# A hybrid decoder layer on one core: eight SSD heads' products in one group, the C and B products of four groups in one, and pairs' transposes moved in front of the next scores

## The chip, the core and the metric

The kernel runs on one core of a Trainium2 chip. Its engines are TensorE (PE, matmuls; PEld is its loading of weights), VectorE (DVE), ScalarE (ACT), GpSimd (POOL) and SyncE (SP, which issues most DMAs). Each engine takes its instructions in the order in which they were issued to it, and waits on semaphores for the others. The metric is the device time of one execution in microseconds (us). Before the change the median of three runs is 745.24 us (745.14 to 746.96).

## The reference

One layer, batch 1, 256 positions, width 1024, float32: a SwiGLU block, then a Mamba-2 (SSD) branch and a differential-attention branch side by side, merged by gates, then a second SwiGLU block. What the change touches is inside the two branches:

```
# SSD: 32 heads of 64, 4 groups of 8 heads, chunks of 128 positions
CB     = einsum('bclgn,bcsgn->bgcls', Cc, Bc)            # per group
y_diag = einsum('bgcls,bgecls,bcsgep->bclgep', CB, Lmat, X)
...
# attention: 8 heads, two maps each, values of 128
p    = softmax(s, axis=-1)
attn = p[:, :, 0] - lam * p[:, :, 1]
out  = einsum('bhqk,bkhe->bqhe', attn, v)
out  = rmsnorm(out, subln_g) * (1.0 - lam_init)
y_att = out @ w_branch
```

The kernel takes the two chunks of the SSD branch as one piece of 256 positions with a causal mask, so that its y is one masked product per head.

## The kernel before

Weights come from HBM in chunks of 1 MB (`load_to`, L140), three raw buffers deep. Each is split into a high and a low part in fp32r: ACT casts (`whi`, L168) and DVE subtracts (`wlo`, L171). `take` (L183) keeps the splits two chunks ahead of PE. Products of weights are three fp32r matmuls for one fp32 product (`mm_t` L197 with 256 columns, 48 passes a tile; `mm_nat` L225 with 512 columns, 12 passes a call). Products inside the branches (`pcb`, `py`, `psc`, `po`) and all transposes are plain fp32 matmuls; each shows as two records on PE.

Buffers come from rings by tag: `k4` (29 tiles of 4 KB a partition: split weights, SSD data, V), `k3` (4: the E of the SSD branch, later the scores `s`), `k2` (7). In PSUM, `pj` (3) serves the weight products and `bg` (5) all else.

The middle of the kernel is woven from two strands. The main strand is the weight products: `pbc` and `pxs` (xs, B and C), `pz`, `pq`/`pk`, then `pgt` (gates), `pws` (the SSD branch's output), `pwd` (the attention's output). The second strand is generators in a queue of class `Background` (L1110): after each main call, `back.run(us)` (L1119) takes steps from them until their `yield` values use up the budget; a `BREAK` ends that round early, and what was saved carries over to the next rounds. Until L1173 a scheduler sets the order of the instructions on all engines. From `own_order(PE)` (L1176) on, PE's order is that of the program; on ACT and DVE the scheduler still decides.

The generators that matter here:

- `cb_work` (L862): for each of four groups, one product of C and B (`pcb`: three blocks of 128 columns, L865 and L866) and one masking multiply on DVE into `cbm` (L867). They run among the `pxs` products.
- `ssd_work` (L875): for each group, transposes of xs (`px`, L881) and a multiply with dt into X (L882). Then for each half of four heads (`hf`): a DMA spreads the decay sums over the partitions (`acb`, L890), two E tiles of two heads each are made on ACT and DVE (L898 to L904), and eight products `py` (L913) of E and X follow, held together on PE by manual dependencies. Each product has 64 output rows, so a head takes half of the array. DVE adds `py` to the scaled xs (L921). So there are eight groups of `py` (16 records each) in all.
- `ssd_norm` (L925): gating, group RMS norm and the split into `yh`/`yl`.
- `att_work` (L1078): eight heads in four pairs, six steps n. Step n does `scores` (L979) and `softmax` (L990) of pair n, `turn` (L1018, transposes `pa` and their copy `aT`) of pair n-1's heads, `combine` (L1006) of pair n, `values` (L1027, six products a pair into `po`) and `norm` (L1045) of pair n-1, and `turn` of pair n-2 (L1057: four transposes `pto` of the normalised pair, then the parts `oh` and `ol`).

`Pair.norm` is a chain over three engines: ACT squares `po` into `o` (L1048), DVE reduces it (L1050) and adds the epsilon term (L1051), ACT takes Ln and Exp (L1053, L1054; shown as L261, the helper), DVE multiplies (L1055). `Pair.turn` on PE reads the `o` that the last of these writes.

## Time and profile before

| what | value |
|---|---|
| runs | 745.14, 745.24, 746.96 us |
| profiled execution | 745.16 us, of which 743.4 us are the span from first to last instruction |
| granted PE clock, mean | 0.997 |
| PE's own chain rows | `acc_f` L470 16%, `pup_f` L219 9%, `pg_f` L219 9%, `pws` L234 6%, `pgt` L234 6% |
| DVE, ACT busy | 71%, 59% of the span |
| costliest DVE and ACT groups | `wlo` L171 290.9 us, `whi` L168 247.2 us |
| SSD products `py`, first to last | 306.6 to 374.6 us |
| pairs' transposes `pto`, first to last | 471.1 to 506.0 us |

The page's first part gives each engine's busy time as a share of the span. The chain follows the work that ended last back to what released it, step by step, and sums it by engine. In the timeline, each row starts with the start time and the duration in us, then the engine, the line, the operation, the tile written and the tiles read, and how many instructions the row joins. Matmuls are pipelined: a row's duration reaches past the start of the next row, so the time that a group costs is read from start to start.

### The profile page before, as it was taken

To read this page: it belongs to the slowest core of one execution; us is meant where nothing else is said; L and a number is where in the kernel's file an instruction comes from. 1 tells how busy PE (TensorE), PEld (TensorE's weight loads), DVE (VectorE), ACT (ScalarE), POOL (GpSimd) and SP (SyncE) were. 2 spreads that over 40 slices of the span, in tenths; PEclk is the share of its full clock that TensorE was granted. 3 is DMA by queue.
4 is the path that set the end of the run, shared out by engine and by line. 5 is a ranking of instruction groups with operands and counts; after the bars stand their busy time and mean duration, and the time that the engine had idled before them with its cause. 6 is when DMAs were issued, how large, how long until landed. Compare 5 with 4: busy or idle time off the path is not lost.

```text
span 743.4 us, 11055 instructions
## 1 busy us (share of the span) xinstructions
PE 734.7 (99%) x4369; PEld 641.3 (86%) x4369; DVE 524.9 (71%) x807; ACT 441.3 (59%) x742; POOL 37.8 (5%) x72
## 2 busy tenths in 40 slices
PE   8999999999999999999999999999999999999996
PEld 6888888888889999999999888888888888888885
DVE  7986567654577888767888998684774867766612
ACT  6665557543566565957967666782664655665512
POOL 2700000000200000000000000000010000000000
PEclk9999999999999999999999999999999999999998
DMA  8884676486253647574656555364470767644701
GB/s 297 225 265 152 206 227 254 174 281 226 64 170 116 202 140 233 168 221 148 197 174 218 173 175 210 127 236 189 135 241 22 226 227 227 190 172 183 277 1 56
DMA packets 94212, 137.96 MB, mean 186 GB/s; under 512 B 2684, under 2 KB 68304, under 8 KB 94160
## 3 DMA queue, kind: packets, MB, share of 16 engines
q1 hardware_dynamic: 91488, 129.51, 52.9%
q0 software_dynamic: 2368, 7.22, 3.2%
q8 instruction: 34, 0.56, 0.3%
q10 hardware_dynamic: 304, 0.53, 0.2%
q14 instruction: 18, 0.15, 0.1%
HBM read 136.17 MB, written 1.08 MB: 185 GB/s over the span
## 4 chain that ended last, share of the span: by engine, by line
PE 98%; DMA 0%; DVE 0%; issue 0%; ACT 0%; DVEq 0%
PE acc_f L470 16%; PE pup_f L219 9%; PE pg_f L219 9%; PE pws L234 6%; PE pgt L234 6%; PE pg_f L218 4%; PE pup_f L218 4%; PE pn_f L244 3%; PE pn_f L234 3%; PE acc_mx L470 3%; PE pn_mx L234 3%; PE pwd L234 3%; PE pz L207 2%; PE pxs L207 2%; PE pz L205 2%; PE pz L204 2%
## 5 line engine op out<-in xcount | busy, mean ns | idle before, releaser
L171 DVE TENSOR_TENSOR wlo<-raw,whi 128x1024 fp32r<-128x1024 f32 (+1 forms) x246 | 290.9, 1211 | 55.7 <-ACT whi L168 54.6
L168 ACT CAST whi<-raw 128x1024 fp32r<-128x1024 f32 (+1 forms) x245 | 247.2, 1047 | 55.3 <-PE acc_f L470 21.7
L219 PE MATMUL pg_f<-u_f,whi 128*128 128x512 f32 x288 | 101.3, 396 | 0.0
L219 PE MATMUL pup_f<-u_f,whi 128*128 128x512 f32 x288 | 101.1, 396 | 0.0
L218 PE MATMUL pg_f<-u_f,wlo 128*128 128x256 f32 x252 | 70.6, 280 | 0.0
L218 PE MATMUL pup_f<-u_f,wlo 128*128 128x256 f32 x252 | 70.3, 279 | 0.0
L219 PEld LDWEIGHTS pg_f<-u_f,whi 128*128 128x128 f32 x288 | 52.8, 188 | 9.7
L219 PEld LDWEIGHTS pup_f<-u_f,whi 128*128 128x128 f32 x288 | 52.7, 188 | 9.8
L470 PE MATMUL acc_f<-whi,gh_f 128*128 128x512 f32 x176 | 58.1, 390 | 0.0
L470 PE MATMUL acc_f<-whi,gl_f 128*128 128x512 f32 x176 | 58.1, 389 | 0.0
L470 PE MATMUL acc_f<-wlo,gh_f 128*128 128x512 f32 x176 | 58.1, 389 | 0.0
L218 PEld LDWEIGHTS pg_f<-u_f,wlo 128*128 128x128 f32 x252 | 47.5, 189 | 1.7
L218 PEld LDWEIGHTS pup_f<-u_f,wlo 128*128 128x128 f32 x252 | 47.5, 189 | 1.6
L223 DVE TENSOR_TENSOR su_f<-pup_f,su_f 128x256 f32<-128x256 f32 x36 | 15.2, 421 | 40.5 <-ACT su_f L222 40.5
L470 PEld LDWEIGHTS acc_f<-wlo,gh_f 128*128 128x128 f32 x176 | 33.0, 188 | 6.9
L470 PEld LDWEIGHTS acc_f<-whi,gl_f 128*128 128x128 f32 x176 | 33.0, 188 | 6.8
L470 PEld LDWEIGHTS acc_f<-whi,gh_f 128*128 128x128 f32 x176 | 33.0, 188 | 6.7
L234 PE MATMUL pgt<-whi,u_mx 128*128 128x512 f32 x128 | 33.1, 393 | 0.0
L222 ACT COPY su_f<-pup_f 128x256 f32<-128x256 f32 x36 | 13.4, 371 | 31.4 <-PE pup_f L219 31.2
L204 PE MATMUL pxs<-u_mx,whi 128*128 128x256 f32 x128 | 31.7, 285 | 0.0
L204 PE MATMUL pz<-u_mx,whi 128*128 128x256 f32 x128 | 31.6, 284 | 0.0
L205 PE MATMUL pz<-u_mx,whi 128*128 128x256 f32 x128 | 31.4, 283 | 0.0
(310 smaller groups left out, 1433.6 us busy)
## 6 DMA issues: line engine op xcount, KB each, us to landing
raw<-in_w_in_dram SPq DMA_DIRECT2D x40, 1024.0 KB, 5.4
raw<-in_ffn_w_down_dram SPq DMA_DIRECT2D x22, 1024.0 KB, 5.1
raw<-in_ffn_w_gate_dram SPq DMA_DIRECT2D x20, 1024.0 KB, 6.0
raw<-in_ffn_w_up_dram SPq DMA_DIRECT2D x20, 1024.0 KB, 5.4
raw<-in_ssd_w_branch_dram SPq DMA_DIRECT2D x8, 1024.0 KB, 5.1
acb<-acd POOLq DMA_DIRECT2D x8, 512.0 KB, 4.9
raw<-in_da_w_branch_dram SPq DMA_DIRECT2D x4, 1024.0 KB, 5.1
raw<-in_w_out_dram SPq DMA_DIRECT2D x4, 1024.0 KB, 4.9
```

The lines of the kernel that those rows point to most:

```text
L168: copy(hi[:, js, :], r[:, q * nj + j:q * nj + j + n, :])
L171: nc.vector.tensor_sub(lo[:, js, :], r[:, q * nj + j:q * nj + j + n, :], hi[:, js, :].bitcast(F32))
L204: nc.tensor.matmul(acc[m], wh(j)[:, cs], ah(k0 + j), start=first and j == ks[0], stop=False)
L205: nc.tensor.matmul(acc[m], wh(j)[:, cs], al(k0 + j), start=False, stop=False)
L207: nc.tensor.matmul(acc[m], wl(j)[:, cs], ah(k0 + j), start=False, stop=last and j == ks[-1])
L218: nc.tensor.matmul(acc[:, :T], wl(j)[:, cs], ah(j), start=False, stop=False)
L219: nc.tensor.matmul(acc, wh(j)[:, cs], ahl(j), start=j == 0, stop=j == KD - 1)
L222: nc.scalar.copy(dst[:, m, :], acc[:, T:])
L223: nc.vector.tensor_tensor(dst[:, m, :], acc[:, :T], dst[:, m, :], ALU.add)
L234: nc.tensor.matmul(acc, a(k0 + j), b(j), start=first and i == 0, stop=last and i == 11)
L244: nc.tensor.matmul(accs[b], x_(k0 + j), w_(j), start=first and j == 0 and w_ is wh and x_ is acts[b][0], stop=last and j == 3 and w_ is wl)
L470: nc.tensor.matmul(acc[b][q], x_[:, ts], w_(kt)[:, halves[q]], start=i == 0 and kt == 0 and x_ is ah and w_ is wh, stop=i == n - 1 and kt ...
```

## The change

Three edits. `cb_work` issues the four groups' products in one go, chained by manual dependencies, into four PSUM tiles, and then does the four multiplies. `ssd_work` makes the E of both halves first and then issues the products of all eight heads of a group, chained, last pair first, with two `py` tiles; the four additions follow, and the `yield` values are 4 x 1.4 and 1.6 instead of 2 x (2 x 1.4 + 0.8). `att_work` runs `turn` of pair n-2 at the start of step n, directly before the scores, instead of at its end; its `yield 0.8` goes, and the yields after each softmax are 2.7 from n = 2 on.

```diff
     def cb_work():
-        for g in range(4):
-            pc = bg([P, 3 * P], f"pcb{g}")
-            nc.tensor.matmul(pc[:, P:], bT[:, g, :P], cT[:, g, :], start=True, stop=True)
-            nc.tensor.matmul(pc[:, :P], bT[:, g, P:], cT[:, g, P:], start=True, stop=True)
+        pcs = [bg([P, 3 * P], f"pcb{g}") for g in range(4)]
+        last = None
+        for g, pc in enumerate(pcs):
+            for m in (nc.tensor.matmul(pc[:, P:], bT[:, g, :P], cT[:, g, :], start=True, stop=True),
+                      nc.tensor.matmul(pc[:, :P], bT[:, g, P:], cT[:, g, P:], start=True, stop=True)):
+                if last is not None:
+                    tc.add_manual_dep(m.ins, last.ins.name, order, reason="together")
+                last = m
+        for g, pc in enumerate(pcs):
             nc.vector.tensor_tensor(cbm[g], pc, m3.rearrange("p a b -> p (a b)"), ALU.mult)
             yield 0.5
...
+            Es = []
             for hf in range(2):
                 acb = k4([P, 4, T], f"acb{g}{hf}")
                 r0 = g * 8 + hf * 4
                 nc.gpsimd.dma_start(acb, acd[r0:r0 + 4, :].partition_broadcast(P))
-                py = bg([P, 2, T], f"py{g}{hf}")
-                Es = []
                 for pr in range(2):
                     E = k3([P, 2, 3 * P], f"E{g}{hf}{pr}")
...
                     yield 1.4

-                last = None
-                for pr in (1, 0):
-                    for keys in range(2):
-                        for i in range(2):
-                            xc = slice((hf * 4 + pr * 2 + i) * 64, (hf * 4 + pr * 2 + i + 1) * 64)
-                            o = py[i * 64:(i + 1) * 64, pr, keys * P:]
-                            m = nc.tensor.matmul(o, X[:, keys, xc], Es[pr][:, i, (1 - keys) * P:(3 - 2 * keys) * P],
-                                                 start=keys == 0, stop=keys == 1)
-                            if last is not None:
-                                tc.add_manual_dep(m.ins, last.ins.name, order, reason="together")
-                            last = m
-                for pr in range(2):
-                    c = hf * 2 + pr
-                    dc = 96 + g * 4 + c
-                    nc.vector.scalar_tensor_tensor(xs[g][:, c, :], xs[g][:, c, :], cols_b[:, dc:dc + 1],
-                                                   py[:, pr, :], ALU.mult, ALU.add)
-                yield 0.8
+            py = [bg([P, 2, T], f"py{g}{hf}") for hf in range(2)]
+            last = None
+            for c in (3, 2, 1, 0):
+                for keys in range(2):
+                    for i in range(2):
+                        xc = slice((c * 2 + i) * 64, (c * 2 + i + 1) * 64)
+                        o = py[c // 2][i * 64:(i + 1) * 64, c % 2, keys * P:]
+                        m = nc.tensor.matmul(o, X[:, keys, xc], Es[c][:, i, (1 - keys) * P:(3 - 2 * keys) * P],
+                                             start=keys == 0, stop=keys == 1)
+                        if last is not None:
+                            tc.add_manual_dep(m.ins, last.ins.name, order, reason="together")
+                        last = m
+            for c in (3, 2, 1, 0):
+                dc = 96 + g * 4 + c
+                nc.vector.scalar_tensor_tensor(xs[g][:, c, :], xs[g][:, c, :], cols_b[:, dc:dc + 1],
+                                               py[c // 2][:, c % 2, :], ALU.mult, ALU.add)
+            yield 1.6
...
             here, old = heads[2 * n:2 * n + 2], heads[2 * n - 2:2 * n] if n else []
+            if n >= 2:
+                pairs[n - 2].turn()
             for head in here:
                 head.scores()
             for head in here:
                 head.softmax()
-                yield 2.3
+                yield 2.3 if n < 2 else 2.7
...
                 yield 1.8
                 if n == H_ATT // 2:
                     yield BREAK
-            if n >= 2:
-                pairs[n - 2].turn()
-                yield 0.8
```

## The prediction

> **What bounds the kernel now.** First the page: busy time and the chain that ended last.

> ```profile
> span 743.4 us, 11055 instructions
> ...
> PE 734.7 (99%) x4369; PEld 641.3 (86%) x4369; DVE 524.9 (71%) x807; ACT 441.3 (59%) x742; POOL 37.8 (5%) x72
> ...
> PE 98%; DMA 0%; DVE 0%; issue 0%; ACT 0%; DVEq 0%
> ```

> PE is busy in 99% of the span and the chain of waits is PE for 98% of it. There is no slack on PE to gain from, and whatever PE waits for newly is added whole. So I read the change as a change of PE's program: what each group of matmuls costs beside its neighbours, and which operand each group would have to wait for. For that I used the timeline of PE, and for the operands the timeline of all engines. PE issues strictly in its order; from before the gate products on, that order is the program's own, written by `own_order(PE)`.

> **SSD heads, eight together.** PE's timeline around the first two `py` groups (columns: start us, duration us, group):

> ```profile
> 306.05 0.52 PE L207 MATMUL pz<-u_mx,wlo 128*128 128x256 f32 x3
> 306.68 1.52 PE L913 MATMUL py<-E,X 128*64 128x256 f32 x16
> 308.13 0.86 PE L207 MATMUL pz<-u_mx,wlo 128*128 128x256 f32 x5
> 308.83 0.28 PE L204 MATMUL pz<-u_mx,whi 128*128 128x256 f32 x1
> ...
> 310.75 1.12 PE L207 MATMUL pz<-u_mx,wlo 128*128 128x256 f32 x8
> 311.80 1.52 PE L913 MATMUL py<-E,X 128*64 128x256 f32 x16
> ```

> An undisturbed f32r pass of 256 columns takes 0.12 (308.83 to 310.75 is 16 of them). After 306.05 three passes need 0.36, so `py` could start at 306.41; it started at 306.68, 0.27 later. After 310.75 eight passes need 0.96, to 311.71; `py` started at 311.80, 0.09 later. So entering the half-array form costs 0.09, and the first group also waited 0.18 for its E. Leaving costs 0.10: five passes from 308.13 to 308.83 take 0.70 instead of 0.60. A group takes 1.45 itself (306.68 to 308.13).

> The next rows give what the same number of fp32 columns takes in the full form:

> ```profile
> 248.84 0.60 PE L865 MATMUL pcb<-cT,bT 128*128 128x256 f32 x2
> 249.28 0.38 PE L866 MATMUL pcb<-cT,bT 128*128 128x128 f32 x2
> 249.42 0.36 PE L204 MATMUL pxs<-u_mx,whi 128*128 128x256 f32 x1
> 249.62 0.28 PE L205 MATMUL pxs<-u_mx,whi 128*128 128x256 f32 x1
> ```

> Two fp32 passes of 256 columns take 0.44, so 0.22 each; one of 128 half of it, 0.11. A `py` group is, two heads side by side, four of each: 1.32. The other 0.13 of its 1.45 are start and drain inside the group. One border less is worth between 0.09 + 0.10 = 0.19 and 0.19 + 0.13 = 0.32; eight groups become four, so 0.8 to 1.3. I take 1.3, since drain belongs to a border, and the old wait of 0.18 at the first group goes too: together -1.5.

> The price is that all four E of a group are held to one point. There are only four `k3` buffers, so the next group's first E waits for the joined matmuls; before, two could be made while two were used. The last E of group 0 sets the new place:

> ```profile
> 310.38 0.96 DVE L904 TENSOR_TENSOR E<-E,cbm 128x768 f32<-128x768 f32 x1 [0.28 <-ACT E L261]
> ```

> It ends at 311.34. The built order of the changed program puts the joined group 11 passes into the fourth `pz` tile, where the second group and 11 passes stood before. Without the early group (1.45 + 0.27 + 0.10) PE reaches that place, entry included, at about 311.3: no wait, or 0.1. From one joined group to the next the changed order has at least 124 passes of 0.12 and eight px transposes of 0.11, 15.8 in all. The SSD stage by engine (columns as named in its head row) and the weight casts in it:

> ```profile
> core 0: us, PE busy (x) PEld busy (x) DVE busy (x) ACT busy (x) POOL busy (x), PEclk, DMA share, GB/s
> ...
> 300.00:380.00 80.00, 79.89 (x689) 75.22 (x689) 62.75 (x99) 64.40 (x125) 3.18 (x6) 1.00 0.57 173
> ```
> ```profile
> L168 ACT CAST whi<-raw 128x1024 fp32r<-128x1024 f32 x22 | 22.2, 1050 | 0.0
> ```

> In the 80 us of the stage DVE works 62.8 and ACT 64.4, and the change neither adds nor removes work on either. Of 15.8 they need 12.4 and 12.7: the E of the next group can be made between two joined groups, with 3 to spare and serially. I take 0.3 for the three later groups together; the bounds are 0 and one cast (1.05) late at each, 3.1.

> **C and B products together.** In the rows of L865 above, two passes of 0.22, two of 0.11 and one f32r pass of 0.12 make 0.78, and 248.84 to 249.62 is 0.78. Neighbours of the full-array form cost nothing to enter or leave, so joining four such groups gains 0. The four products on DVE come earlier; what hides them is the rest of the xs products, since only the E of the next stage read them, and of five `bg` buffers they take four while nothing else asks for one. Without that cover PE would wait for one mask product on DVE, a 384-column operation: under 0.7, by the 512-column multiply of `norm` below.

> **Pairs' transposes ahead of the scores.** The gain first. They are full-array fp32, so they leave PE for free; the scores' own entry remains (they use half of the rows). The gain is 0. The cost is in the moved place. Before, `pairs[n - 2].turn()` ran at the end of step n, a whole step after `norm` had begun. Now it runs at the start of step n, right behind step n-1's `values` and `norm` of that same pair. In the built order of the changed program PE has between a pair's last value product and its transposes: 12 `pws` passes for pair 0, nothing for pair 1, nothing for pair 2, 12 for pair 3. PE then waits for Square, reduce, two small steps, Ln, Exp, and the last multiply. All engines, pair 0:

> ```profile
> 450.74 0.39 PE L1036 MATMUL po<-v,aT 128*128 128x128 f32 x2
> ...
> 451.16 0.60 ACT L1048 ACTIVATE o<-po 128x512 f32<-128x512 f32 x1 [0.70 <-PE po L1036]
> 451.29 1.22 DVE L171 TENSOR_TENSOR wlo<-raw,whi 128x1024 fp32r<-128x1024 f32 x1
> ...
> 452.42 0.68 DVE L1050 TENSOR_REDUCE ro<-o 128x4 f32<-128x512 f32 x1
> ...
> 453.81 0.69 DVE L1055 TENSOR_TENSOR o<-po,ro 128x512 f32<-128x512 f32 x1 [0.51 <-ACT ro L261]
> ...
> 453.82 0.50 PE L987 MATMUL psc<-k,q 64*128 64x128 f32 x4
> ```

> From the reduction's start (452.42) to the normalised pair (453.81 + 0.69 = 454.50) the chain runs back to back: 2.08. PE, after its 12 passes, started scores at 453.82, of which 0.09 is entry: the transposes could start at 453.73. They get their operand at 454.50, and I add 0.1 for the hand-over and weight load (estimate; PE to ACT takes 0.03 here, 451.13 to 451.16). Wait: 0.9. Without the split that DVE does first (451.29) it would be 0.3.

> Pair 1, whose value products end at 471.41, with another pair's transposes then directly behind:

> ```profile
> 470.85 1.23 DVE L171 TENSOR_TENSOR wlo<-raw,whi 128x1024 fp32r<-128x1024 f32 x1 [5.98 <-ACT whi L168]
> ...
> 471.02 0.39 PE L1036 MATMUL po<-v,aT 128*128 128x128 f32 x2
> ...
> 471.24 0.60 PE L1061 MATMUL pto<-ident,o 128*128 128x128 f32 x4
> 471.44 0.60 ACT L1048 ACTIVATE o<-po 128x512 f32<-128x512 f32 x1 [0.62 <-PE po L1036]
> ...
> 472.07 0.69 DVE L1050 TENSOR_REDUCE ro<-o 128x4 f32<-128x512 f32 x1
> ```

> Square ends at 472.04, the reduction starts at 472.07, so the bare chain is ready at 472.07 + 2.08 + 0.1 = 474.25, and PE would have started at 471.24: 3.0. That is pair 2's price. For pair 1 the changed order puts a split `wlo` (1.23, as at 470.85) before the reduction, and that split writes the buffer of V's first half, which the last value product has just read: it starts at 471.44, the reduction at 472.67, and the wait is 3.6. Pair 3:

> ```profile
> 502.59 0.60 PE L1061 MATMUL pto<-ident,o 128*128 128x128 f32 x4
> ...
> 502.79 0.69 DVE L1217 TENSOR_TENSOR gt<-pws,gt 128x512 f32<-128x512 f32 x1
> ...
> 503.39 0.68 DVE L1055 TENSOR_TENSOR o<-po,ro 128x512 f32<-128x512 f32 x1
> ```

> The slot after its 12 passes is 502.59 (before, pair 2's transposes stood there); its own operand was ready at 503.39 + 0.68. With the 0.1: 1.6. It cannot shrink much, since the multiply of `gt` (502.79) ends the same 12 passes' tile and stands ahead of the last multiply on DVE in both programs.

> Waits: 0.9 + 3.6 + 3.0 + 1.6 = 9.1; bounds 0.3 + 3.0 + 3.0 + 1.4 = 7.7 (no other DVE work ahead) and 11.5 (one more split of 1.2 ahead for pairs 1 and 2). Behind PE's wait stand the scores of the next two heads (behind pair 2's, the last heads' transposes) and then `pws`; DVE and ACT wait for those with softmax, evictions and the casts that reuse the weights' buffers. Nothing later is short of anything, so no later wait takes the time back.

> **The clock.** A PE pause of 3 us is new to this kernel. Two places show what idling and starting do: the end (columns: us, busy time and count by engine, then PEclk),

> ```profile
> 737.00:739.20 2.20, 0.25 (x2) 0.00 (x0) 1.19 (x2) 1.19 (x4) 0.00 (x0) 1.00 0.00 0
> 739.20:743.40 4.20, 0.00 (x0) 0.00 (x0) 0.82 (x2) 0.00 (x0) 0.00 (x0) 0.50 0.33 125
> ```

> and the start:

> ```profile
> 1.59 1.65 PE L310 MATMUL warm<-ident 128*128 128x128 f32 x6 [1.59 <-POOL ident L296]
> ...
> 3.72 1.86 PE L355 MATMUL pu_f<-ident,h 128*128 128x128 f32 x8 [0.28 <-DMA h<-in_x_dram]
> 5.42 0.61 PE L310 MATMUL warm<-ident 128*128 128x128 f32 x4
> ```

> PE ended at 737.25 and its clock was at 0.50 from 739.20: 1.95 later. At the start eight transposes took 0.21 each (3.72 to 5.42), twice the 0.11 of 128 columns above; the four at 5.42 take 0.61 with their tail, so less than 4 x 0.21: half clock from 1.59 until about 5.4, 3.8 of work, or 1.9 lost. So waits of 3.0 and 3.6 should each halve the clock, those of 0.9 and 1.6 perhaps not. A fall costs between 0 and 1.9; some of the slow stretch passes while PE still waits, so I take 1.4 each, 2.8.

> [...]

> **Sum.** -1.3 - 0.2 + 0.3 + 9.1 + 2.8 = +10.7 on the profiled execution's 745.16 (span 743.4 and 1.76 around it): 755.9. The median of the runs is 745.24, so nothing has to be added for that.

> **Rivals.**
> 1. Waits as said, clock stays full: 755.9 - 2.8 = 753.1. For it: only two transitions were ever recorded. Against: 1.95 at the end. Chance 0.22.
> 2. Not slower: the pair's norm keeps up with PE. One mechanism: PE's waits at the four transposes are 0 because `o` is ready when PE arrives; it decides once 2.8 us or more of PE work stand between value products and transposes. Then 745.16 - 1.5 + 0.3 = 744.0, no change by measurement (0.3%, 2.2 us, is about what can be told apart here). Against: the built order shows nothing between them for pairs 1 and 2. Chance 0.04. Even the change's full gain (1.5) is no measurable gain, so faster has 0.01.
> 3. The joined groups also stall: E of groups 1 to 3 come a cast late each, and PE waits 2.8 more: 758.7. For it: ACT has 3 of 15.8 spare, and four buffers serialise it. Chance 0.10.
> The forecast has 0.62; 0.02 stays for what I don't see.

> **Numbers.** 755.9. Range 751.3 (waits at 7.7, clock full, merging at its best) to 760.5 (an extra split ahead of one reduction, a clock that recovers late, some late E). It holds the forecast and rivals 1 and 3. Slower: 0.62 + 0.22 + 0.10 + 0.02 = 0.96; same 0.03; faster 0.01.

> **What would show it.** PE idle rows before `pto` of about 0.9, 3.6, 3.0 and 1.6, released by the last multiply of `norm` on DVE; half-clock stretches after the second and third of them, with 512-column passes of twice 0.23; four `py` groups of 32 matmuls with no idle above 0.3 before them; the C and B rows unchanged in sum. Wrong would be: `pto` without idle (rival 2), PEclk 1.00 throughout (rival 1), idle before `py` (rival 3), or PE time lost outside these places, above all before `pxs`, where DVE's order changes too.

## The result, and the profile after

The changed kernel takes 757.34 us (median of four runs, 757.17 to 760.27); the kernel before, run beside it, 745.63 (745.14 to 746.96). The ratio is 1.017, with a 95% interval of 1.0157 to 1.0182: slower by 1.7%. The profiled executions are 757.22 after and 745.16 before, 12.06 apart, and so are their spans. The page of the kernel after, first part and chain:

```profile
span 755.5 us, 11064 instructions
...
PE 737.2 (98%) x4369; PEld 643.6 (85%) x4369; DVE 525.8 (70%) x807; ACT 441.4 (58%) x742; POOL 38.0 (5%) x72
...
PE 96%; DVE 2%; DMA 1%; ACT 1%; issue 0%; SPq 0%; DVEq 0%
```

The number of PE records is the same, PE is busy 2.5 us longer, and 9.6 of the 12.06 us are idle PE time: by the rows below, 8.9 at the waits for the pairs' transposes and most of the rest at the start of the program. In the chain the other engines, almost absent before, now hold 4%. The table of waits of the kernel after says what PE stood for (columns: us in all, times, longest):

```profile
PE pto L1065 <- DVE o L1059: 8.9, 4, 4.0
PE warm L310 <- POOL ident L296: 1.6, 1, 1.6
PE pn_f L244 <- ACT raw_u L361: 1.1, 1, 1.1
```

The second and third rows are at the start of the program and there before as well (the third with 0.3). The first is new: four waits, one for each pair, for the last multiply of its `norm`. The PE timeline of the kernel after shows them one by one (each first row is the work just before):

```profile
452.28 1.08 PE L234 MATMUL pws<-whi,yl 128*128 128x512 f32 x4
454.02 0.66 PE L1065 MATMUL pto<-ident,o 128*128 128x128 f32 x4 [0.66 <-DVE o L1059]
...
474.48 0.39 PE L1040 MATMUL po<-v,aT 128*128 128x128 f32 x2
...
478.85 0.63 PE L1065 MATMUL pto<-ident,o 128*128 128x128 f32 x4 [3.98 <-DVE o L1059]
...
500.88 0.39 PE L1040 MATMUL po<-v,aT 128*128 128x128 f32 x2
504.08 1.12 PE L1065 MATMUL pto<-ident,o 128*128 128x128 f32 x4 [2.81 <-DVE o L1059]
504.99 1.49 PE L1026 MATMUL pa<-ident,s 128*128 128x128 f32 x6
...
512.58 1.08 PE L234 MATMUL pws<-whi,yl 128*128 128x512 f32 x4
515.13 0.63 PE L1065 MATMUL pto<-ident,o 128*128 128x128 f32 x4 [1.47 <-DVE o L1059]
```

Read from start to start, less what the passes of the row ahead need (0.23 each for 512 columns of f32r: twelve take 2.73 from 470.63 to 473.36; 0.11 each for 128 of fp32: ten take 1.12 from 473.36 to 474.48), PE loses 0.82, 4.15, 2.97 and 1.63 there, together 9.57. The bracket counts from the modelled end of the previous matmul and so shows a little less.

The clock, by the stretches of the kernel after (columns: busy us and count by engine, then PEclk, DMA share, GB/s):

```profile
core 0: us, PE busy (x) PEld busy (x) DVE busy (x) ACT busy (x) POOL busy (x), PEclk, DMA share, GB/s
472.87:476.28 3.41, 2.00 (x15) 1.68 (x13) 3.41 (x4) 2.02 (x3) 0.00 (x0) 1.00 0.39 77
476.28:479.70 3.42, 0.85 (x8) 0.72 (x10) 1.88 (x4) 0.60 (x3) 0.00 (x0) 1.00 1.00 361
479.70:483.11 3.41, 3.41 (x18) 2.51 (x16) 2.26 (x5) 1.31 (x2) 0.00 (x0) 0.50 0.46 178
500.18:503.59 3.41, 1.09 (x10) 0.90 (x9) 1.40 (x4) 1.01 (x3) 0.00 (x0) 1.00 0.92 312
503.59:507.00 3.41, 2.92 (x12) 2.83 (x13) 1.18 (x2) 1.60 (x3) 0.00 (x0) 0.50 0.05 13
```

The clock is halved twice, each time for 3.41 us, from 479.70 and from 503.59, and in both PE had work again for most of the time: pair 2's four transposes take 0.91 there (504.08 to 504.99 in the timeline above), 0.23 each instead of 0.11.

The joined groups of the SSD stage, PE timeline of the kernel after:

```profile
311.98 0.28 PE L204 MATMUL pz<-u_mx,whi 128*128 128x256 f32 x1
312.28 2.82 PE L918 MATMUL py<-E,X 128*64 128x256 f32 x32
315.03 1.09 PE L886 MATMUL px<-ident,xs 128*128 128x128 f32 x8
...
330.71 0.28 PE L204 MATMUL pz<-u_mx,whi 128*128 128x256 f32 x1
330.92 2.82 PE L918 MATMUL py<-E,X 128*64 128x256 f32 x32
333.67 0.39 PE L205 MATMUL pz<-u_mx,whi 128*128 128x256 f32 x1
```

Four such groups stand where eight stood. Each takes 2.75 from its start to the next row's (312.28 to 315.03). The first starts 0.30 after the pass before it, that is 0.09 late beyond that pass (0.12) and the border (0.09); the second 0.21 after it, with no wait at all.

To see where the 12.06 us arise, I compared the same PE instruction in both traces at several places: the table gives by how much it starts later after the change.

| place | start, before | start, after | later by |
|---|---|---|---|
| first `pn_f` of the first block | 6.31 | 7.03 | 0.72 |
| first `pxs` | 243.08 | 243.81 | 0.73 |
| first `pz` (C and B done) | 291.75 | 292.64 | 0.89 |
| last `pk` stage done, first `pgt` | 401.02 | 400.49 | -0.53 |
| last `pwd` (attention done) | 528.72 | 540.77 | 12.06 |
| end of the span | 743.4 | 755.5 | 12.06 |

So 0.7 lie at the very start, before anything that the change touches: there the first weights came later in this execution (the first cast waits for its DMA until 6.46 instead of 5.74), and the kernels of the experiments differ among themselves by about as much. Joining C and B costs 0.16, the SSD stage gains 1.42, and attention costs 12.59. After it nothing is taken back and nothing is added.

### The profile page after: what moved, and what is told of

It is laid out like the page before. It is cut to its first block, busy times and chain, and to the rows that moved or that the text cites. A ratio compares the mean times of both kernels' runs of the same rounds, so it can differ in the third digit from the quotient of the medians.

```text
span 755.5 us, 11064 instructions
## 1 busy us (share of the span) xinstructions
PE 737.2 (98%) x4369; PEld 643.6 (85%) x4369; DVE 525.8 (70%) x807; ACT 441.4 (58%) x742; POOL 38.0 (5%) x72
## 4 chain that ended last, share of the span: by engine, by line
PE 96%; DVE 2%; DMA 1%; ACT 1%; issue 0%; SPq 0%; DVEq 0%
PE acc_f L470 16%; PE pup_f L219 9%; PE pg_f L219 9%; PE pgt L234 6%; PE pws L234 6%; PE pg_f L218 4%; PE pup_f L218 4%; PE pn_f L244 3%; PE pn_f L234 3%; PE acc_mx L470 3%; PE pn_mx L234 3%; PE pwd L234 3%; PE pz L205 2%; PE pxs L204 2%; PE pxs L207 2%; PE pxs L205 2%
## 5 line engine op out<-in xcount | busy, mean ns | idle before, releaser
L171 DVE TENSOR_TENSOR wlo<-raw,whi 128x1024 fp32r<-128x1024 f32 (+1 forms) x246 | 291.0, 1212 | 59.8 <-ACT whi L168 59.5
L168 ACT CAST whi<-raw 128x1024 fp32r<-128x1024 f32 (+1 forms) x245 | 246.5, 1045 | 58.7 <-PE acc_f L470 21.6
L205 PE MATMUL pz<-u_mx,whi 128*128 128x256 f32 x128 | 31.6, 284 | 0.0
L204 PE MATMUL pz<-u_mx,whi 128*128 128x256 f32 x128 | 31.6, 284 | 0.0
L204 PE MATMUL pxs<-u_mx,whi 128*128 128x256 f32 x128 | 31.5, 284 | 0.0
```

What stands on the lines that cost most here:

```text
L168: copy(hi[:, js, :], r[:, q * nj + j:q * nj + j + n, :])
L171: nc.vector.tensor_sub(lo[:, js, :], r[:, q * nj + j:q * nj + j + n, :], hi[:, js, :].bitcast(F32))
L204: nc.tensor.matmul(acc[m], wh(j)[:, cs], ah(k0 + j), start=first and j == ks[0], stop=False)
L205: nc.tensor.matmul(acc[m], wh(j)[:, cs], al(k0 + j), start=False, stop=False)
```

## The experiments

Seven kernels were run, each beside the kernel before. Besides the times I compared the traces at the same places as above, which removes the differences at the start; "attention" below is the growth between the first `pgt` and the last `pwd` against the kernel before.

**1 (e1_no_turn_move). The turns back in their old place, the SSD and C/B edits kept.**

```diff
-            if n >= 2:
-                pairs[n - 2].turn()
...
-                yield 2.3 if n < 2 else 2.7
+                yield 2.3
...
+            if n >= 2:
+                pairs[n - 2].turn()
+                yield 0.8
```

> The changed kernel with the pairs' transposes back at the end of a step (yields as before), the SSD and the C and B products joined. My theory: the loss is the moved transposes alone, so PE idles nowhere in the attention part and the clock stays at 1.00 from about 5 us to the end of the matmuls; 745.2 - 1.4 (joined SSD groups) + 0.2 (a wait at the joined C and B products that the trace of the changed kernel shows) = 744.0. Rival (joined SSD groups or joined C and B products cost more than they save): not below 745.2.

Measured: 744.03 us against 745.14 before, ratio 0.9984 (0.9976 to 0.9993). The trace has the C/B step at +0.16, the SSD stage at -1.41 and attention at 0.00. The loss belongs to the third edit alone, and without it the change is a small gain.

**2 (e2_turn_move_alone). The moved turns alone, on the kernel before.**

```diff
+            if n >= 2:
+                pairs[n - 2].turn()
...
-                yield 2.3
+                yield 2.3 if n < 2 else 2.7
...
-            if n >= 2:
-                pairs[n - 2].turn()
-                yield 0.8
```

> The kernel before with the moved transposes and their yields alone. My theory: the four waits (9.6 in the trace of the changed kernel) and two stretches at half clock (3.1) come with it: 745.2 + 12.7 = 757.9, PE idle before pto near 0.8, 4.1, 3.0 and 1.6. Rival (the waits come from DVE and ACT running late because of the joined SSD groups): waits near their bare chains, 0.3, 3.0, 3.0 and 1.4, and below 756.

Measured: 757.53 us (756.42 to 759.16), ratio 1.016 (1.0142 to 1.0179). The four waits are the same ones (0.82, 4.14, 2.97 and 1.63), yet attention grew by 11.18 instead of 12.59. The stretches around pairs 1 and 2 of this kernel tell why:

```profile
476.50:479.91 3.41, 0.12 (x1) 0.16 (x2) 2.60 (x5) 0.41 (x2) 0.00 (x0) 1.00 0.97 351
479.91:483.32 3.41, 3.41 (x20) 2.65 (x19) 0.94 (x2) 0.69 (x1) 0.00 (x0) 0.50 0.66 253
500.39:503.80 3.41, 1.78 (x14) 1.50 (x13) 1.82 (x3) 0.65 (x2) 0.00 (x0) 1.00 0.97 319
503.80:507.22 3.42, 2.25 (x15) 2.08 (x16) 1.44 (x2) 1.80 (x5) 0.00 (x0) 1.00 0.22 85
```

Here pair 2's pause lies across two stretches of 3.41 us, counted on from the fall at 479.91 (502.16 to 504.97: PE is idle for 48% of the one and 34% of the other), and the clock stays at 1.00. The same pause in the kernel after lies mostly in one (68%), and the clock falls. One fall less is 1.4 us less. The runs of one kernel differ in this too: kernel 2 took 756.42 and 756.79 us at a mean granted clock of 0.996, 758.26 at 0.994 and 759.16 at 0.992. One halved stretch of 3.41 us takes 0.002 off that mean (half of 3.41 in a span of 755.1), so this fits one and two falls more, though only the run of 756.79 has a trace.

**3 (e3_pause_filled). The pauses of pairs 1 and 2 filled with matmuls that nobody reads.** It adds 23 identity products into the tile that the transposes then overwrite.

```diff
             pt = bg([P, 4, P], f"pto{hp}")
+            for _ in range({1: 14, 2: 9}.get(hp, 0)):
+                nc.tensor.matmul(pt[:, 0, :], ident, ident, start=True, stop=True)
```

> The changed kernel with idle matmuls of the identity put into the wait: 14 before pair 1's transposes and 9 before pair 2's, 0.22 each (3.1 and 2.0), written to the tile that the transposes then overwrite. The waits still end when the normalised pair is there, so PE gets nothing done sooner. Theory of the clock: pauses of 1.0 to 1.1 are left, PEclk stays 1.00 and the time falls by what the two slow stretches cost, 3.1, to 754.2. Rival (the slow stretches cost nothing of their own, the waits are longer instead): 757.3, unchanged.

Measured: 753.37 us (753.28 to 753.7), ratio 1.0104 (1.0089 to 1.012). The clock is 1.00 around both pauses (474 to 481 and 498 to 505 us), and attention grew by 9.56, which is the sum of the four waits (9.57) in the kernel after. So the pauses and the slow clock are two costs: the first is 9.6, and the second is what the kernel after has on top, 12.59 - 9.56 = 3.0.

**4 (e4_one_call_between). One call of `pws` (12 passes) between a pair's norm and its transposes.**

```diff
             if n >= 2:
+                yield BREAK
                 pairs[n - 2].turn()
```

> The changed kernel with one break ahead of each moved turn, so that one more call of 12 passes (2.7) stands between a pair's value products and its transposes. Theory: each wait shrinks by 2.7: pair 0 and pair 3 to 0, pair 1 from 4.1 to 1.4, pair 2 from 3.0 to 0.3; no pause is long enough for the clock. 744.0 + 1.7 = 745.7. Rival (DVE's queue grows with PE's passes, so that the chain ends as late after the extra call): waits as before the edit, 757.

Measured: 757.62 us (756.32 to 758.57), ratio 1.0159 (1.0141 to 1.0176). I expected 745.7 and missed by 12. Pairs 0 and 3 have no wait any more, but pair 1 waits 6.1 us and pair 2 2.9, with 2.85 us of passes in front of both (473.45 to 476.30 at pair 1). DVE's timeline of this kernel around pair 1 (its value products end at 473.45):

```profile
473.07 3.50 DVE L171 TENSOR_TENSOR wlo<-raw,whi 128x1024 fp32r<-128x1024 f32 x3 [7.10 <-ACT whi L168]
476.48 0.68 DVE L1221 TENSOR_TENSOR gt<-pws,gt 128x512 f32<-128x512 f32 x1
477.08 1.21 DVE L171 TENSOR_TENSOR wlo<-raw,whi 128x1024 fp32r<-128x1024 f32 x1
478.22 0.68 DVE L1054 TENSOR_REDUCE ro<-o 128x4 f32<-128x512 f32 x1
478.81 0.68 DVE L1221 TENSOR_TENSOR gt<-pws,gt 128x512 f32<-128x512 f32 x1
479.41 0.15 DVE L1055 SCALAR_TENSOR_TENSOR ro<-ro,eps 128x4 f32<-128x4 f32 x1
479.48 2.35 DVE L171 TENSOR_TENSOR wlo<-raw,whi 128x1024 fp32r<-128x1024 f32 x2
481.75 0.68 DVE L1059 TENSOR_TENSOR o<-po,ro 128x512 f32<-128x512 f32 x1
```

The chain is not what takes the time: of the 8.7 us from 473.70 (last value product out of the array) to 482.43, `norm` needs 0.6 for Square on ACT and 2.1 for the five steps from the reduction on. DVE had been idle for 7.10 us, waiting for weight casts that ACT could not make while it loaded tables (1.28, twice) and took four sigmoids of the gates (3.91). Then three splits, a gate multiply and a fourth split stand ahead of the reduction. And behind the reduction, but ahead of the chain's last multiply, DVE's order has a gate multiply, which evicts the very call that I had put in, and two splits issued later still. The call covers 2.85 us, and what joins the queue with it takes 2.9 (478.81 to 479.41 and 479.48 to 481.75). That is not all: from the start of the last two value products to the transposes it now takes 9.26 us (473.31 to 482.57) instead of 4.37 in the kernel after (474.48 to 478.85). Of the growth, 2.12 lie behind the start of the reduction, and 2.77 ahead of it, where the same five DVE instructions as in the kernel after now come later behind the value products. The clock was halved over two stretches after each wait (PEclk 0.50 from 480.36 to 487.18 at pair 1; at pair 2 the transposes at 508.40 take 0.22 each, and passes of 512 columns 0.46 from 510.42 and still 0.43 from 512.27), and attention grew by 14.3.

**5 (e5_groups_joined_alone). The joined SSD groups alone, on the kernel before** (the second hunk of the change, and no other edit).

```diff
-                py = bg([P, 2, T], f"py{g}{hf}")
-                Es = []
...
+            py = [bg([P, 2, T], f"py{g}{hf}") for hf in range(2)]
...
+            yield 1.6
```

> The kernel before with the joined value products of the eight SSD heads alone; the C and B products and the pairs' turns stay where they were. Theory: the joined groups give the whole gain of the SSD part, four borders less at .32 us and the old waits, so TensorE reaches the end of that stage 1.3 to 1.6 us earlier than before, and the span ends 1.3 to 1.6 us earlier (time 743.7, within .4). Rival 1: the joining of the C and B products is what pays, then this kernel is at 745.1 as before. Rival 2: the joined groups stall on their last E, then it is 745.4 or more, with a wait on E of over .3 us at each group.

Measured: 744.0 us, ratio 0.9986 (0.9977 to 0.9995). The SSD stage gains 1.43 in the trace, with no PE wait on E in its table of waits, and the C/B step changes by 0.00 where the kernels with joined C and B have +0.16. Rivals 1 and 2 fall. The times of kernels 1 and 5 are not to be told apart.

**6 (e6_norm_ahead_on_DVE). Kernel 4 with the norm ahead of younger work on DVE and ACT.** `behind` adds a dependency of order on the norm's multiply (DVE) or its Exp (ACT) to each later split, cast and gate multiply.

```diff
+    def behind(m, engine):
+        if chain:
+            tc.add_manual_dep(m.ins, chain[engine], order, reason="behind a pair's norm")
...
-                copy(hi[:, js, :], r[:, q * nj + j:q * nj + j + n, :])
+                behind(copy(hi[:, js, :], r[:, q * nj + j:q * nj + j + n, :]), 1)
...
-            act(r, r, AF.Exp, scale=-0.5)
-            nc.vector.tensor_tensor(self.o, po, r.unsqueeze(2).to_broadcast([P, 4, P]), ALU.mult)
+            e = act(r, r, AF.Exp, scale=-0.5)
+            m = nc.vector.tensor_tensor(self.o, po, r.unsqueeze(2).to_broadcast([P, 4, P]), ALU.mult)
+            chain[:] = [m.ins.name, e.ins.name]
```

> The kernel of e4_one_call_between, with VectorE's weight splits and gate multiplies, and ScalarE's weight casts, that are issued after a pair's norm ordered behind that norm's own work. In e4 PE waited 6.1 us at pair 1 and 2.9 us at pair 2, although 12 passes stood between. Theory: there the norm's last multiply stood behind two splits (2.35 us), a gate multiply (.68 us) and, at pair 2, casts between Ln and Exp; with these behind it, pair 1's wait is 3.8 us (three splits, one gate multiply and one split issued earlier stay ahead) and pair 2's .4 us, 4.2 us in all instead of 9.0, and at most one fall of the clock: 744.0 + 4.2 + 0 to 2.5 = 748.2 to 750.7. Rival: the queue of VectorE doesn't matter and one call is too short for the chain itself: waits of 9 us again and 757.6.

Measured: 751.03 us (749.83 to 751.56), ratio 1.0072 (1.0056 to 1.0087). One wait is left, at pair 1, of 4.0 us; pair 2's is gone. Same passes on PE, 6.6 us less: the order on DVE and ACT was the cause of that part. At pair 1 of kernel 4 it was DVE's, since ACT stood idle for 1.33 us before Ln, waiting for DVE; at pair 2 casts on ACT also stood ahead of Ln and of Exp (504.21 and 505.27). In DVE's timeline of this kernel the norm now runs together, behind the same three splits, one gate multiply and one split as before, which the edit leaves ahead of the reduction:

```profile
478.36 0.68 DVE L1062 TENSOR_REDUCE ro<-o 128x4 f32<-128x512 f32 x1
479.07 0.16 DVE L1063 SCALAR_TENSOR_TENSOR ro<-ro,eps 128x4 f32<-128x4 f32 x1
479.74 0.69 DVE L1067 TENSOR_TENSOR o<-po,ro 128x512 f32<-128x512 f32 x1 [0.51 <-ACT ro L268]
480.35 0.68 DVE L1230 TENSOR_TENSOR gt<-pws,gt 128x512 f32<-128x512 f32 x1
```

The time is 0.3 above the upper end that I gave. Attention grew by 7.12: a PE pause of 4.14 and a slow clock from 479.74 on (PEclk 0.51 from 479.70 to 483.11, 0.50 from 479.91 to 483.32). It is slow for longer than one stretch of 3.41: the four score passes from 483.46 to 484.62 take 1.16, those of kernel 7 from 481.90 to 482.53 take 0.63. Two stretches would end at 486.56, so that PE worked 5.98 us at the slow clock after its pause had ended (an estimate from these rows). Half of that is 2.99, and 4.14 + 2.99 = 7.13.

**7 (e7_two_calls_between). Two calls (24 passes) between, DVE's order left to the scheduler.**

```diff
             if n >= 2:
+                yield BREAK
+                yield BREAK
                 pairs[n - 2].turn()
```

> As e4_one_call_between, but with two products' calls (24 passes, 6.6 us) between a pair's values and its transposes. Theory: a call of 3.3 us brings VectorE up to 4.6 us of splits and gate work ahead of pair 1's norm, so one call doesn't help, but the second call brings no more ahead of it: from the first split at pair 1 8.4 us of VectorE work end 1.2 us after the 24 passes, a wait of 1.2 us (0 to 2.5), pair 2 none, no fall of the clock: 744.0 + 1.2 = 745.2 (744.0 to 746.5). Rival: each call brings more of VectorE's work than it covers, so that the wait stays over 6 us at pair 1 and 3 us at pair 2, with falls of the clock: 757 or more.

Measured: 745.87 us (745.68 to 746.27), ratio 1.0005 (0.9996 to 1.0014). PE's waits in attention are 1.1 us at pair 1 and, new, 0.3 at a `pwd` call that reads pair 3's parts; the mean granted clock is 0.998, and attention grew by 1.86. The 24 passes take 5.58 us here (473.53 to 479.11), not the 6.6 of the expectation. But more than the distance has changed. DVE's timeline around pair 1:

```profile
474.85 1.23 DVE L171 TENSOR_TENSOR wlo<-raw,whi 128x1024 fp32r<-128x1024 f32 x1 [1.62 <-ACT whi L168]
476.00 0.68 DVE L1054 TENSOR_REDUCE ro<-o 128x4 f32<-128x512 f32 x1
476.59 2.35 DVE L171 TENSOR_TENSOR wlo<-raw,whi 128x1024 fp32r<-128x1024 f32 x2
...
479.54 0.68 DVE L1059 TENSOR_TENSOR o<-po,ro 128x512 f32<-128x512 f32 x1
```

One split stands ahead of the reduction, where kernel 4 had four and a gate multiply, and the chain ends 6.4 us after the last value product left the array (473.78 to 480.22) instead of 8.7. With the 9.26 us of kernel 4, 24 passes would have left a wait of about 3.5 (an estimate: 9.26 less 0.14 and 5.58). So two calls, with the queue that the scheduler then makes, hide this norm but for 1.1 us; what the distance alone does was not measured.

## Why the prediction held, point by point

- **The place and the mechanism.** The four idle stretches, their releaser and their place are as forecast, and kernels 1 and 2 show that the moved turns alone make the loss. The forecast was 755.9, the time is 757.3.
- **The waits, 9.1 forecast, 9.57 found.** Pair 0 0.9 and 0.82, pair 2 3.0 and 2.97, pair 3 1.6 and 1.63. The mis-sized term is pair 1: "the wait is 3.6", from one split ahead of the reduction. It is 4.15. DVE's timeline of the kernel after:

```profile
471.48 3.50 DVE L171 TENSOR_TENSOR wlo<-raw,whi 128x1024 fp32r<-128x1024 f32 x3 [6.63 <-ACT whi L168]
474.89 0.69 DVE L1220 TENSOR_TENSOR gt<-pws,gt 128x512 f32<-128x512 f32 x1
475.49 1.22 DVE L171 TENSOR_TENSOR wlo<-raw,whi 128x1024 fp32r<-128x1024 f32 x1
476.62 0.68 DVE L1054 TENSOR_REDUCE ro<-o 128x4 f32<-128x512 f32 x1
```

  The split that I counted is there (475.49), and a gate multiply (0.60 to the next start) as well. Three splits behind the late casts keep DVE busy until 474.89, so that the multiply and that split stand wholly in front of the reduction. The lateness of the casts could be read in the trace before (5.98 idle, released by ACT); I used that row only for the length of one split.
- **The clock, 2.8 forecast, 3.0 found.** It did fall twice, once at each of the two long waits. Kernel 3 gives the price by taking the falls away. That the two falls are both there is partly luck: kernel 2 has the same waits and one fall. The row on which the forecast leaned, 1.95 us at the end of the kernel before, did not bear the step to "each": of the stretches of 3.41 us at full clock read in the last section, those with 58% or more of idle PE were followed by a fall and those with 48% or less were not, and that row's stretch, with 58%, is the lowest that was. Rival 1 falls.
- **The SSD groups, -1.5 + 0.3 forecast, -1.42 found.** Two old groups took 2 x 1.45 = 2.90, a joined one 2.75, so the drain inside is 0.15 less, and with one entry of 0.09 and one exit of 0.10 less a join is worth 0.34: four are 1.36, where 1.3 was taken. The old wait of 0.18 at the first group became 0.09. This makes 1.45; one of the four exits removed led into `px`, where leaving costs 0.05 and not 0.10 (the first `px` pass takes 0.16 instead of 0.11), which makes it 1.40. The 0.3 for late E was too careful: the three later groups have no wait. Rival 3 falls.
- **C and B, 0 forecast, +0.16 found.** PE timeline of the kernel after, where all eight rows stand together:

```profile
249.58 0.60 PE L866 MATMUL pcb<-cT,bT 128*128 128x256 f32 x2
...
250.66 0.38 PE L867 MATMUL pcb<-cT,bT 128*128 128x128 f32 x2
250.91 0.70 PE L866 MATMUL pcb<-cT,bT 128*128 128x256 f32 x2
251.45 0.38 PE L867 MATMUL pcb<-cT,bT 128*128 128x128 f32 x2
251.67 0.60 PE L866 MATMUL pcb<-cT,bT 128*128 128x256 f32 x2
```

  The third product loses 0.14: it starts 0.25 after the last row instead of 0.22, and its two passes take 0.54 to the next start instead of 0.43. It is found in each kernel with joined C and B and in no other. Its weight load starts together with it, at 250.91, where the loads of the second and fourth start 0.11 ahead of their products; what that load waits for the trace doesn't name, so the cause stays open.
- **Rival 2's condition was wrong,** though the rival fell anyway. It said that the waits vanish "once 2.8 us or more of PE work stand between". Kernel 4 has 2.85 between and keeps 9 us of waits. The 2.8 is the chain's own length on idle engines. What decides is the queue in which the chain's steps stand: kernel 6 changes the order alone and takes 6.6 us off. In kernel 7 the distance and the queue changed together.
- **The rest, 757.22 against a sum of 745.16 - 1.42 + 0.16 + 12.59 = 756.5,** is the 0.7 at the start of that execution.

## What to carry to other kernels

When a step is moved closer to its producer on an engine that is never idle, price the producer's chain in the queues in which it stands, not by itself: here a chain of 2.7 us took up to 8.7, because splits and an eviction, some of them younger, stood ahead of its steps on VectorE. In this kernel a pause of TensorE that is about 3 us long could cost more than itself: half of the work done at the slow clock after it came on top (2.99 of 5.98 us in kernel 6, an estimate). Whether it did went with where the pause lay: with 68% of one stretch of 3.41 us idle the clock fell (kernel after), with 48% and 34% of two it did not (kernel 2), after a wait of 2.97 us in both. Of an edit in several parts, run each alone: here the joined SSD groups alone make 744.0, 0.14% below the kernel before (interval 0.05% to 0.23%), and the third part hid it.

## What the runs showed of the hardware

The share of idle PE is what PE's busy time leaves of a stretch. In attention, the clock fell behind stretches at full clock with 75% (from 476.28) and 68% (from 500.18) in the kernel after, 96% in kernel 2 (from 476.50), 100% (from 476.94) and 62% (2.11 of 3.41 us from 504.25) in kernel 4, and 92% in kernel 6 (from 476.33). It stayed at 1.00 behind 41% (from 472.87) and 38% (from 513.83) in the kernel after, and 48% and 34% in kernel 2 (from 500.39 and 503.80). At the end of the kernel before, PE was idle for 1.97 of the 3.42 us from 735.80 (58%), and the clock is halved from 739.22. In the profiled execution of kernel 1 the mean granted clock is 0.999, against 0.997 there, so it fell later (an estimate from the two means).

A halved clock came back after one stretch with 0% of idle PE (kernel 2 from 479.91, the kernel after from 479.70) or 14% (the kernel after from 503.59), and not after one with 65% or 22% (kernel 4, from 480.36 and 507.66) or 25% (kernel 6, from 479.74), where it lasted into a second stretch. So a pause of 2.81 us cost the clock in the kernel after and not in kernel 2, and a pause that reached 0.74 us or more into the next stretch cost more than one (2.21 and 0.74 in kernel 4, 0.84 in kernel 6), one that reached 0.49 into it cost one (pair 2 in the kernel after). What sets the clock beyond these readings was not measured.
